# Differential attention normed without 1/sum, its last heads spread over the output projection, and some operands moved by 32 bytes

## The chip, the core and the metric

One NeuronCore of a Trainium2 chip runs the whole program. The metric is device microseconds (us) from start to end of one execution; a kernel's time is the median of several. The engines are named as in the profile: PE is TensorE (PEld its weight loads), DVE is VectorE, ACT is ScalarE, POOL is GpSimd, SP issues the transfers.

## What is computed

A block of three layers over 256 positions of width 1024: a convolution layer, a differential-attention layer (both followed by a cross attention to 256 memory tokens and a SwiGLU of hidden width 2816), then a layer of another kind. The change touches the second layer's attentions and two of the SwiGLUs. Cut to what matters:

```python
# diff_attention: 8 heads, two softmaxes of 64 wide halves, value width 128
p = softmax(where(mask, s, -inf))                 # s = q k / 8, c = 0, 1
a = p[:, :, 0] - lam * p[:, :, 1]
o = einsum('bhqk,bkhe->bqhe', a, v)
o = rms_norm(o, subln_g, 1e-5) * (1.0 - lambda_init)   # per head, over its 128 values
x = x + o.reshape(B, S, 1024) @ w_o

# memory_cross_attention: 4 heads of 256
p = softmax(q k / 16);  o = p @ v;  x = x + o @ w_o

# swiglu
x = x + (silu(h @ w_gate) * (h @ w_up)) @ w_down
```

The norm of a head does not change when the head is multiplied by a positive factor, except through the 1e-5: with unnormed exponentials `e` and their sum `s0` for c = 0, `o = u / s0`, and `o * rsqrt(mean(o^2) + 1e-5)` is `u * rsqrt(mean(u^2) + 1e-5 * s0^2)`.

## The kernel before

**Weights.** Every weight matrix passes as panels of 128 rows by up to 1024 columns. SP loads a panel into `wf` (6 buffers); ACT copies it to `whi` (line 276, the high part in fp32r) and DVE or POOL subtracts, `wlo = wf - whi` (line 278). `whi` and `wlo` have 5 buffers each. Which engine makes `wlo` is told for each matrix by the table `LO`, one letter for each panel in turn (`g` is POOL, `v` is DVE). `consume()` prepares panels up to 5 ahead of the one in use, so a panel's `whi` waits until PE is done with the panel 5 before it.

**Products.** `gemm` (line 409 holds its matmul) multiplies activations, also split into a high and a low part (`S0`, `S1` or `hh`), by the panels: three matmuls for each product, high by high, low by high, high by low. In the form "F" the panel is the stationary operand and 256 positions of the activations stream; in the form "T" the activations are stationary and 512 columns of the panel stream. A panel serves 4 banks of 6 matmuls each. The last `tail` panels are held back and done bank by bank, so that each bank's result can be drained (`evac`) while the next is computed. `hooks` run other work after a given panel.

**Differential attention** is written out in an order by hand. `q` is the projection of two heads, `V` that of the values, `a` the scores and exponentials of a head, `b` the combination of its two halves and its transposes (PE lines 897), `c` the product with the values (lines 906 to 908), and `f` the norm of a pair of heads and its transposes into `S0` (`fin`, lines 913 to 930). `DIFF_SEQ` stands ahead of the output projection; `DIFF_END` hangs the rest on it as hooks: `a6 c4` after panel 0, `a7 c5 b6` after panel 1, `b7 f2 c6 c7 f3` after panel 3. Panels 4 to 7 (`TAIL = 4`) are the held ones. Panel `k` of `w_o` needs head `k`, so panels 4 and 5 need `f2`, panels 6 and 7 `f3`.

In `fin`, four steps on DVE around a power on POOL (line 920) make the factor, DVE multiplies the heads by it (line 925, two instructions of 128x256), and PE transposes (line 928). In the memory attention `b_` DVE scales the exponentials by 1/sum (line 708, two instructions) before PE's transposes (line 712).

**The norm of the layer's input** is applied late: `Stats` adds squares on POOL (line 338), folds them (line 355) and PE sums them over the partitions (line 361). In the projection to `k` (`w_ks`) that sum is asked for after panel 4.

**Where operands lie.** Start addresses in a partition, in bytes, as the built program has them:

| tile | role | start before | modulo 64 |
|---|---|---|---|
| s0h, s0l, s1h, s1l | streaming in form F, stationary in T | 32128, 40320, 48512, 56704 | 0 |
| whi, wlo (10 buffers) | stationary in F, streaming in T | 92256 to 129120 | 32 |
| hh, hl of the first two SwiGLUs | streaming against whi, wlo | 148064, 170592 | 32 |
| hh, hl of the third SwiGLU | stationary, whi and wlo stream | 161408, 183936 | 0 |
| q against memory K; pT against memory V | q stationary, K streams; V stationary, pT streams | all | 32 |

## Time and profile before

| | |
|---|---|
| median of 3 runs | 1169.73 us (1169.61 to 1170.72) |
| the profiled execution's own time | 1166.55 us |
| its span in the profile | 1164.8 us |
| mean granted clock of PE | 0.983 |
| PE busy | 1114.5 us of the span (96%) |
| DVE, ACT, POOL busy | 788.7, 650.2, 426.2 us |

The stages in the order of the span: convolution and memory projections to 182 us, first memory attention to 245, first SwiGLU to 433 (its down projection from 370), differential attention to 559, second memory attention to 623, second SwiGLU to 811 (down projection from 747), then the other layer, whose SwiGLU runs from 973 to the end. Busy shares of the whole span are averages over these; what a part of the change is worth is read in its own stage.

### The profile page before, as it was taken

Reading aid. Unit: us, or ns where it says so; the run is one execution under the profiler, and the core shown is the slowest. Engines: PE = TensorE matmul, PEld = TensorE weight load, DVE = VectorE, ACT = ScalarE, POOL = GpSimd, SP = SyncE. Lnnn points to the kernel's source line nnn. Section 1 sums busy time; section 2 is a strip of 40 time slices with the busy share of each in tenths; the row PEclk is TensorE's granted clock in tenths of the full one; section 3 lists DMA queues with packets and bytes.
Section 4 is the critical chain, followed back from the end, with each engine's and each line's share of the span. In section 5 each row is a group of like instructions: output and inputs, shape, how many; then the busy total and the mean of one; then the engine's idle time right before and its main releaser. Section 6 shows DMA issues by size and latency. Waiting matters only on the chain.

```text
span 1164.8 us, 21545 instructions
## 1 busy us (share of the span) xinstructions
PE 1114.5 (96%) x8418; PEld 1055.0 (91%) x8418; DVE 788.7 (68%) x1445; ACT 650.2 (56%) x1141; POOL 426.2 (37%) x278
## 2 busy tenths in 40 slices
PE   7999989999999999988999999999988998999997
PEld 7998878999999998978899999999887678999986
DVE  6899866596767456675855565745868746887843
ACT  6555476565545355654755554535675745765642
POOL 5999846220000016763726444001663310111300
PEclk9999989999999999998999999999998998999999
DMA  7676535356546544542434654753654015455661
GB/s 265 193 246 206 196 112 179 109 160 207 182 145 235 183 147 165 177 145 73 145 109 134 229 182 149 234 188 102 208 184 160 19 55 176 150 200 155 226 198 37
DMA packets 59799, 191.13 MB, mean 164 GB/s; under 512 B 6752, under 2 KB 10080, under 8 KB 59696
## 3 DMA queue, kind: packets, MB, share of 16 engines
q1 hardware_dynamic: 58288, 187.31, 49.3%
q0 software_dynamic: 688, 1.90, 0.6%
q8 instruction: 66, 1.08, 0.4%
q10 hardware_dynamic: 720, 0.53, 0.1%
q14 instruction: 37, 0.30, 0.1%
HBM read 188.15 MB, written 1.05 MB: 162 GB/s over the span
## 4 chain that ended last, share of the span: by engine, by line
PE 45%; DVE 2%; issue 2%; POOL 1%; ACT 0%; POOLq 0%; DVEq 0%; ACTq 0%
PE acc L409 38%; PE acc L1120 1%; PE acc L1218 1%; PE acc L723 0%; POOL sacc L338 0%; DVE wlo L278 0%; PE acc L1279 0%; PE acc L1283 0%; PE aux L1260 0%; PE acc L1372 0%; PE acc L1280 0%; PE acc L1215 0%; PE acc L1170 0%; POOL sfold L355 0%; PE acc L692 0%
## 5 line engine op out<-in xcount | busy, mean ns | idle before, releaser
L276 ACT ACTIVATE whi<-wf 128x1024 fp32r<-128x1024 f32 (+3 forms) x382 | 371.2, 986 | 310.8 <-PE acc L409 270.2
L278 DVE TENSOR_TENSOR wlo<-wf,whi 128x1024 fp32r<-128x1024 f32 (+3 forms) x251 | 317.5, 1274 | 177.2 <-ACT whi L276 176.3
L278 POOL TENSOR_TENSOR wlo<-wf,whi 128x1024 fp32r<-128x1024 f32 (+1 forms) x131 | 286.9, 2209 | 167.9 <-ACT whi L276 167.6
L409 PE MATMUL acc<-s0h,whi 128*128 128x256 f32 x1192 | 340.0, 286 | 6.0 <-ACT whi L276 5.4
L409 PE MATMUL acc<-s0h,wlo 128*128 128x256 f32 x1192 | 336.9, 283 | 3.4 <-POOL wlo L278 3.4
L409 PE MATMUL acc<-s0l,whi 128*128 128x256 f32 x1192 | 336.6, 283 | 1.7 <-DVE s0l L435 1.7
L409 PEld LDWEIGHTS acc<-s0h,whi 128*128 128x128 f32 x1192 | 228.4, 192 | 7.1 <-ACT whi L276 5.4
L409 PEld LDWEIGHTS acc<-s0h,wlo 128*128 128x128 f32 x1192 | 227.8, 191 | 4.7 <-POOL wlo L278 4.5
L409 PEld LDWEIGHTS acc<-s0l,whi 128*128 128x128 f32 x1192 | 228.3, 192 | 2.7 <-DVE s0l L435 2.1
L409 PE MATMUL acc<-s1h,whi 128*128 128x256 f32 x736 | 205.8, 281 | 0.7 <-ACT s1h L649 0.7
L409 PE MATMUL acc<-s1h,wlo 128*128 128x256 f32 x736 | 205.5, 279 | 0.9 <-POOL wlo L278 0.5
L409 PE MATMUL acc<-s1l,whi 128*128 128x256 f32 x736 | 205.5, 279 | 0.3 <-DVE s1l L435 0.3
L409 PEld LDWEIGHTS acc<-s1h,whi 128*128 128x128 f32 x736 | 138.1, 188 | 1.7 <-ACT s1h L649 1.4
L409 PEld LDWEIGHTS acc<-s1h,wlo 128*128 128x128 f32 x736 | 138.3, 188 | 1.3 <-POOL wlo L278 0.7
L409 PEld LDWEIGHTS acc<-s1l,whi 128*128 128x128 f32 x736 | 138.4, 188 | 0.8 <-DVE s1l L435 0.5
L409 PE MATMUL acc<-hh,whi 128*128 128x256 f32 x352 | 99.6, 283 | 0.0
L409 PE MATMUL acc<-hl,whi 128*128 128x256 f32 x352 | 99.6, 283 | 0.0
L409 PE MATMUL acc<-hh,wlo 128*128 128x256 f32 x352 | 99.6, 283 | 0.0
L338 POOL TENSOR_TENSOR sacc<-sq,sacc 128x512 f32<-128x512 f32 x21 | 33.5, 1596 | 122.4 <-ACT sq L337 122.0
L543 DVE SCALAR_TENSOR_TENSOR aux<-u,vecs,aux 128x256 f32<-128x256 f32 x174 | 68.6, 476 | 1.1 <-ACT aux L541 1.1
L409 PEld LDWEIGHTS acc<-hh,wlo 128*128 128x128 f32 x352 | 67.6, 192 | 0.0
L409 PEld LDWEIGHTS acc<-hl,whi 128*128 128x128 f32 x352 | 67.6, 192 | 0.0
(371 smaller groups left out, 1720.2 us busy)
## 6 DMA issues: line engine op xcount, KB each, us to landing
wf<-in_gu SPq DMA_DIRECT2D x120, 512.0 KB, 3.9
wf<-in_w_down SPq DMA_DIRECT2D x66, 512.0 KB, 4.3
wf<-in_mem_w_k SPq DMA_DIRECT2D x16, 512.0 KB, 4.2
wf<-in_mem_w_v SPq DMA_DIRECT2D x16, 512.0 KB, 3.4
wf<-in_mem_w_q SPq DMA_DIRECT2D x16, 512.0 KB, 3.5
wf<-in_mem_w_o SPq DMA_DIRECT2D x16, 512.0 KB, 4.2
wf<-in_w_pw SPq DMA_DIRECT2D x24, 256.0 KB, 3.1
wf<-in_gv SPq DMA_DIRECT2D x24, 256.0 KB, 2.7
```

What stands on the lines that cost most here:

```text
L276: p["ih"] = SC.activation(p["hi"][:, :W], p["f"][:, :W], AF.Copy)
L278: p["il"] = eng.tensor_tensor(p["lo"][:, :W], p["f"][:, :W], p["hi"][:, :W].bitcast(F32), op=OP.subtract)
L338: self.ins = self.eng.tensor_tensor(self.acc, sq, self.acc, op=OP.add)
L409: PE.matmul(o, l, r, start=(ki == 0 and n == 0 and q == 0), stop=(ki == K - 1 and q == 2), skip_group_check=True)
L543: V.scalar_tensor_tensor(cv[:, c] if k == TAPS - 1 else ai, src, w, ai, op0=OP.mult, op1=OP.add)
L1120: PE.matmul(ph[0:60, 0:256], win[:, a, 4 * g + j], w[:, j * 256:(j + 1) * 256], start=(g == 0 and j == 0 and w is p["hi"]), stop=(g == 3 a ...
L1218: PE.matmul(f, q1, kk[:, kv], start=True, stop=True, skip_group_check=True)
```

## The change

Five things are edited. (1) `b_` of the differential attention keeps `e0 = 1e-5 * s0^2` in the place of `r0 = 1/s0`; `fin` takes one DVE step ahead of the power in the place of three, none behind it, and ACT scales the heads (four instructions of 128x128) in the place of DVE. (2) `DIFF_END` spreads the last heads: `c6` after panel 2, `f2 b7` after bank 1 of panel 3, `c7` after bank 0 of panel 4, `f3` after bank 1 of panel 5; two panels are held in the place of four. (3) The low parts of `w_o` and of the first `q` go from POOL to DVE. (4) In the second memory attention ACT scales the exponentials by 1/sum, in the place of DVE. (5) A tile `pad` of 32 bytes heads the pools of both memory attentions and of the first two SwiGLUs: hh and hl then start at 148096 and 170624 (0 modulo 64), q and pT at 0 modulo 64, while the memory K and V, whi and wlo stay at 32 modulo 64. The first memory attention keeps its scaling on DVE.

```diff
-DIFF_END = {0: "a6 c4", 1: "a7 c5 b6", 3: "b7 f2 c6 c7 f3"}
+DIFF_END = {0: "a6 c4", 1: "a7 c5 b6", 2: "c6", (3, 1): "f2 b7", (4, 0): "c7", (5, 1): "f3"}
...
-          dn0="v", K="v", q="g", V="g", o="g", mq1="gvv", mo1="vgv", gu1="gv", gv1="v",
+          dn0="v", K="v", q="g", V="g", o="v", mq1="gvv", mo1="vgv", gu1="gv", gv1="v",
...
-            declare("w_q", 2 * int(w[1]), 2, nk=4, lo=LO["q"])
+            declare("w_q", 2 * int(w[1]), 2, nk=4, lo="v" if w == "q0" else LO["q"])
...
                 for b in range(len(banks)):
                     mm(ki, cur, b)
+                    for f in hooks.get((ki, b), []):
+                        f()
...
             P = es.enter_context(tc_pool(name=f"ma{i}", bufs=3))
+            V.memset(P.tile([128, 8], F32, name="pad", bufs=1), 0.0)
             P1 = es.enter_context(tc_pool(name=f"mq{i}", bufs=1))
             if i:
+                V.memset(P1.tile([128, 8], F32, name="pad"), 0.0)
...
                 for t in range(2):
-                    V.tensor_scalar(p[:, t], p[:, t], sm[:, 2 + t:3 + t], None, op0=OP.mult)
+                    if i:
+                        SC.activation(p[:, t], p[:, t], AF.Copy, scale=sm[:, 2 + t:3 + t])
+                    else:
+                        V.tensor_scalar(p[:, t], p[:, t], sm[:, 2 + t:3 + t], None, op0=OP.mult)
...
             P = es.enter_context(tc_pool(name=f"ff{i}", bufs=1))
+            V.memset(P.tile([128, 8], F32, name="pad"), 0.0)
...
-            V.reciprocal(r0[:, :, h], sm[:, 0, 0:2])
+            V.scalar_tensor_tensor(e0[:, :, h], sm[:, 0, 0:2], 1e-5, sm[:, 0, 0:2], op0=OP.mult, op1=OP.mult)
...
-            V.tensor_tensor(ms, ss[:, :, hs], r0[:, :, hs], op=OP.mult)
-            V.tensor_tensor(ms, ms, r0[:, :, hs], op=OP.mult)
-            V.tensor_scalar(ms, ms, 1.0 / 128, 1e-5, op0=OP.mult, op1=OP.add)
+            V.scalar_tensor_tensor(ms, ss[:, :, hs], 1.0 / 128, e0[:, :, hs], op0=OP.mult, op1=OP.add)
             rr = small.tile([128, 2, 2], F32, name="orr", tag="orr")
             G.tensor_tensor(rr, ms, mhalf[:, 0:4].rearrange("p (a b) -> p a b", a=2), op=OP.pow)
-            V.tensor_tensor(rr, rr, r0[:, :, hs], op=OP.mult)
             pt = acc()
             for t in range(2):
-                ov = o[:, t, 256 * g:256 * g + 256].rearrange("p (h e) -> p h e", h=2)
-                V.tensor_tensor(ov, ov, rr[:, t, :, None].to_broadcast([128, 2, 128]), op=OP.mult)
                 for i in range(2):
                     h = 2 * g + i
+                    ov = o[:, t, h * 128:(h + 1) * 128]
+                    SC.activation(ov, ov, AF.Copy, scale=rr[:, t, i:i + 1])
                     PE.transpose(pt[:, i * S + t * 128:i * S + (t + 1) * 128], o[:, t, h * 128:(h + 1) * 128], ident)
...
-             hooks={k: [lambda w=w: run(w.split())] for k, w in DIFF_END.items()}, tail=TAIL)
+             hooks={k: [lambda w=w: run(w.split())] for k, w in DIFF_END.items()}, tail=2)
```

A scheduler lays the instructions of each engine in a row; line numbers below 660 grow by 2, those of `fin` by about 5. On POOL, from the last adds of squares of the first SwiGLU through the differential attention (`sacc`, `sfold` and `rr` are the norm of the input, `orr` the power in `fin`), the row before is:

```order
L338 TENSOR_TENSOR sacc<-sq,sacc 128x512 x2
L278 TENSOR_TENSOR wlo<-wf,whi 128x1024
L338 TENSOR_TENSOR sacc<-sq,sacc 128x512
L355 TENSOR_TENSOR sfold<-sacc 128x256
L372 TENSOR_TENSOR rr<-ms,mhalf 128x2
L278 TENSOR_TENSOR wlo<-wf,whi 128x1024 x14
L920 TENSOR_TENSOR orr<-oms,mhalf 128x4
L278 TENSOR_TENSOR wlo<-wf,whi 128x1024 x4
L920 TENSOR_TENSOR orr<-oms,mhalf 128x4
```

and now, to the last `orr`:

```order
L338 TENSOR_TENSOR sacc<-sq,sacc 128x512 x3
L355 TENSOR_TENSOR sfold<-sacc 128x256
L372 TENSOR_TENSOR rr<-ms,mhalf 128x2
L278 TENSOR_TENSOR wlo<-wf,whi 128x1024 x13
L926 TENSOR_TENSOR orr<-oms,mhalf 128x4
L278 TENSOR_TENSOR wlo<-wf,whi 128x1024
L926 TENSOR_TENSOR orr<-oms,mhalf 128x4 x2
L278 TENSOR_TENSOR wlo<-wf,whi 128x1024
L926 TENSOR_TENSOR orr<-oms,mhalf 128x4
```

The low part between the adds is gone, and so are the eight of `w_o` around the powers; one, of the next matrix, stands ahead of the last power.

On ACT, from a square of `c5` (`sqs`) to the start of the drain of `w_o` (`s1h`), with `pT` the copy of `b7` and `s0h` the high part that `f2` and `f3` write, the row before is:

```order
L910 ACTIVATE sqs,ss<-aux 128x128
L276 ACTIVATE whi<-wf 128x1024 x2
L899 ACTIVATE pT<-aux 128x384
L929 ACTIVATE s0h<-acc,subg 128x512
L910 ACTIVATE sqs,ss<-aux 128x128 x4
L929 ACTIVATE s0h<-acc,subg 128x512
L434 ACTIVATE s1h<-acc,vecs 128x256 x3
```

and now, behind the first two scalings of `f2` (`o`), to the last one of `f3`:

```order
L276 ACTIVATE whi<-wf 128x1024
L918 ACTIVATE sqs,ss<-aux 128x128
L932 ACTIVATE o<-o,orr 128x128
L918 ACTIVATE sqs,ss<-aux 128x128
L932 ACTIVATE o<-o,orr 128x128
L934 ACTIVATE s0h<-acc,subg 128x512
L907 ACTIVATE pT<-aux 128x384
L276 ACTIVATE whi<-wf 128x1024
L918 ACTIVATE sqs,ss<-aux 128x128 x2
L932 ACTIVATE o<-o,orr 128x128 x3
L276 ACTIVATE whi<-wf 128x1024
L932 ACTIVATE o<-o,orr 128x128
```

The scalings have come in, and weight copies and the squares of `c6` stand among them.

## Rows read from the trace of the kernel before

**Rows 1.** The page, part 1: busy time, share and instructions of each engine.
```profile
PE 1114.5 (96%) x8418; PEld 1055.0 (91%) x8418; DVE 788.7 (68%) x1445; ACT 650.2 (56%) x1141; POOL 426.2 (37%) x278
```
**Rows 2.** Stretches: length, busy us (count) PE, PEld, DVE, ACT, POOL; PE clock; DMA, GB/s.
```profile
269.00:369.00 100.00, 100.00 (x860) 100.00 (x859) 66.55 (x88) 51.31 (x70) 0.00 (x0) 1.00 0.54 175
370.00:433.00 63.00, 63.00 (x527) 63.00 (x526) 32.32 (x35) 27.17 (x34) 0.00 (x0) 1.00 0.57 185
83.00:105.00 22.00, 22.00 (x96) 17.74 (x95) 21.87 (x51) 11.85 (x16) 21.92 (x11) 1.00 0.62 202
516.60:558.80 42.20, 35.89 (x260) 34.34 (x260) 27.41 (x63) 19.02 (x51) 15.24 (x8) 0.88 0.22 76
```
**Rows 3.** The chain that ended last, second memory attention: start, us, what.
```profile
584.85 5.61 PE acc L409 x48
...
590.46 1.43 PE acc L692 x12
...
603.37 1.43 PE acc L723 x12
```
**Rows 4.** Instructions in order of time, POOL, then PE, `w_ks`: start, us, idle before.
```profile
445.82 2.38 POOL L278 TENSOR_TENSOR wlo<-wf,whi 128x1024 fp32r<-128x1024 f32 x1 [0.36 <-ACT whi L276]
448.17 1.25 POOL L338 TENSOR_TENSOR sacc<-sq,sacc 128x512 f32<-128x512 f32 x1
449.50 0.72 POOL L355 TENSOR_TENSOR sfold<-sacc 128x256 f32<-128x256 f32 x1
...
450.28 0.60 PE L361 MATMUL aux<-ones,sfold 128*128 128x1 f32 x4 [2.76 <-POOL sfold L355]
```
**Rows 5.** Instructions in order of time around `w_o`: POOL, DVE, PE, then ACT.
```profile
515.26 2.49 POOL L278 TENSOR_TENSOR wlo<-wf,whi 128x1024 fp32r<-128x1024 f32 x1 [0.34 <-ACT whi L276]
...
515.42 2.94 DVE L925 TENSOR_TENSOR o<-o,orr 128x256 f32<-128x256 f32 x2
...
539.61 2.91 DVE L925 TENSOR_TENSOR o<-o,orr 128x256 f32<-128x256 f32 x2
...
548.94 0.76 DVE L925 TENSOR_TENSOR o<-o,orr 128x256 f32<-128x256 f32 x2
...
518.17 0.68 PE L928 MATMUL acc<-cst,o 128*128 128x128 f32 x4 [1.23 <-DVE o L925]
...
521.12 0.99 PE L897 MATMUL aux<-cst,p 128*128 128x128 f32 x3 [1.94 <-DVE p L892]
...
542.58 0.69 PE L928 MATMUL acc<-cst,o 128*128 128x128 f32 x2 [2.04 <-DVE o L925]
...
545.92 0.28 ACT L910 ACTIVATE sqs<-aux 128x128 f32<-128x128 f32 x1 [0.51 <-PE aux L908]
...
546.50 0.19 ACT L910 ACTIVATION_READ_ACCUMULATOR sqs<-aux 128x1 f32 x1
```
**Rows 6.** Single microseconds of PE: length, busy (count), granted clock, DMA, GB/s.
```profile
522.00:523.00 1.00, 1.00 (x7) 0.50 0.95 381
...
545.00:546.00 1.00, 1.00 (x6) 0.50 0.05 21
```
**Rows 7.** Instructions in order of time, first softmax of the second memory attention: DVE, PE.
```profile
581.84 2.41 DVE L708 TENSOR_SCALAR p<-p,sm 128x256 f32<-128x256 f32 x2
...
584.04 0.81 PE L712 MATMUL aux<-cst,p 128*128 128x128 f32 x4 [3.57 <-DVE p L708]
```
**Rows 8.** Groups by line and shape: busy us, mean ns of one, idle before.
```profile
L276 ACT ACTIVATE whi<-wf 128x1024 fp32r<-128x1024 f32 x314 | 327.6, 1058 | 266.7 <-PE acc L409 233.3 <-issue 22.4 <-POOL wlo L278 4.3
L278 DVE TENSOR_TENSOR wlo<-wf,whi 128x1024 fp32r<-128x1024 f32 x215 | 286.7, 1342 | 160.9 <-ACT whi L276 159.9
...
L788 ACT ACTIVATE t<-t 128x256 f32<-128x256 f32 x44 | 18.2, 414 | 12.3 <-DVE t L787 11.8
...
L452 ACT ACTIVATE x<-acc 128x512 f32<-128x512 f32 x20 | 11.9, 597 | 0.0
...
L920 POOL TENSOR_TENSOR orr<-oms,mhalf 128x4 f32<-128x4 f32 x4 | 4.1, 1028 | 10.7 <-DVE oms L918 10.7
```

More of the change, by code (lines that the diff above doesn't have):

```diff
@@ L861, in program @@
         B = {}
-        r0 = P1.tile([128, 2, 8], F32, name="r0")
+        e0 = P1.tile([128, 2, 8], F32, name="e0")
         ss = P1.tile([128, 2, 8], F32, name="ss")
```

## The prediction

> **What bounds the kernel now.** I read the page's busy times first: PE works in 96% of the span, no other engine in more than 68% [rows 1]. Only two things can then move the end: the time PE takes for a matmul, and the few stretches in which PE stands idle or slow. For the first I read stretches of pure matmul [rows 2]. In the gate and up part of the first SwiGLU 860 matmuls of 256 columns take 100 us, 116.3 ns each; in its down projection 527 of the same shape take 63 us, 119.5 ns each. In both, PE is busy throughout at a granted clock of 1.00, so the 3.3 ns are no wait. The operands lie differently: `hh` streams at 32 modulo 64 against `whi` at 32, while the faster stretch streams tiles at 0 against the same `whi`. The chain of waits has the same pair once more [rows 3]: 48 matmuls of the projection take 5.61 us (116.9 ns each), while the two memory-attention products, both operands at 32, take 1.43 us for 12 (119.2 ns each). For the second I read the output projection of the differential attention as one stretch: PE is busy for 35.89 of 42.20 us at a mean clock of 0.88 [rows 2]. Then the instructions in order of time give each idle time its releaser [rows 4, 5, 7].
>
> **Operands moved by 32 bytes.** Each pair that has both operands at 32 now has one at 0 and one at 32. With the tile at 0 streaming that is the faster stretch; with the tile at 0 stationary and the panel at 32 streaming (the new way round for the memory V or K against q and pT included), 96 matmuls of 512 columns take 22 us, 229 ns each, under two of the fast 256-column ones [rows 2]. So I take the full difference: two down projections of 22 panels by 4 banks by 6 are 1056 matmuls by 3.26 ns, 3.4 us; two memory attentions with 4 heads of 24 are 192 by 2.3 ns, 0.4 us. **Gain 3.8 us.** Bounds: 0, if another cause than the address slows these stretches, and 4.1 if the fast stretch's edges are counted in. The `pad` memsets are tiny and stand on DVE, which is idle for a third of the span [rows 1]; they cost nothing while PE has queued matmuls, and some 0.2 us each if not. The Trainium skill speaks against this gain (rivals).
>
> **Low parts moved from POOL: the norm of the layer's input.** PE waits 2.76 us for the fold before it sums over the partitions [rows 4]. On POOL's row a `wlo` of 2.38 us stands between the last two adds and pushes the second, of 1.25, and the fold, of 0.72, behind it. Without it, the add can start when its squares are there instead. POOL had been kept from it for at most the 2.38, and the squares that release it come later than the `wlo`'s start, so I take half: **gain 1.2 us**, bounds 0 and 2.76. What is late next is that add itself, and the `wlo`, now on DVE: 1.34 us of it [rows 8] beside POOL, with DVE free there.
>
> **The output projection.** What is there to win: 42.20 − 35.89 = 6.3 us idle, of which 1.23, 1.94 and 2.04 stand in front of `f1`, `b5` and the second half of `f2` [rows 5]; and the clock, (1 − 0.88) × 42.2 × 0.85 busy = 4.3 us. The microseconds at half clock, 7 and 6 matmuls in each in the place of 8.6, come right after `f1` with `b5` and after `f2` [rows 2, 6], behind those idle times. The pair of DVE scalings takes 2.94 and 2.91 us beside a `wlo` on POOL, 0.76 us at `f3` [rows 5]: so sharing with POOL, not the work, made DVE late, and both causes go (no `wlo` of `w_o` on POOL, no scaling on DVE). What is put in their place I add up by laying the new rows of PE, ACT and POOL against one another:
> - `f1`: the power, 1.03 us [rows 8], then the scalings of 128x128, 0.28 each by the square of that shape [rows 5]. 0.7 us of PE's wait stays; `b5`'s exponentials aren't behind the scaling any more, so 1.94 goes.
> - `f2` on ACT's row: power 1.03, four scalings 1.1, a `whi` of 1.06 [rows 8] and a square pair between, 0.6: 3.8 us. PE has 12 matmuls of panel 3 and the first transposes over it, 1.7. Wait 2.1.
> - `f3`: squares of `c7` 0.77 (545.92 to 546.69) [rows 5], power 1.03, four scalings 1.1, two `whi` 2.1, DVE's step and the handovers some 0.7: 5.7 us, with 30 matmuls (3.5 us) between `c7` and `f3`. Wait 2.2.
> - The drain: with two held panels a bank has 12 matmuls, 1.4 us, in the place of 2.8; ACT needs about 2 × 0.41 + 2 × 0.60 = 2.0 for a bank [rows 8]. PE, which goes on with the next matrix, waits 0.8 at the last ones.
> - Smaller waits that I find in the same comparison: 0.5 at the rotation of `q3`, 0.45 at `b6` and `c6`, 0.5 for the low part that follows `f2` and `f3`. None lasts long enough to slow the clock by what `f1` before shows, where the loss came behind 1.23 and 1.94 in a row.
>
> Together 7.25 us. I take the clock as full. **Gain 6.3 + 4.3 − 7.25 = 3.4 us**, bounds −1 (clock lost again) and 8 (ACT finds cover for both). Eight low parts of `w_o`, 1.34 us each, go on DVE, which is busy for 27.4 of 42.2 us there [rows 2]; they fit, if they don't stand ahead of what PE waits for (third rival). Queued behind ACT's scalings is the `whi` of the next panels, and PE behind that has several panels ready.
>
> **The scaling in the second memory attention.** The pair takes DVE 2.41 us at the first head, and PE waits 3.57 in all for it [rows 7]. ACT does 128x256 in 0.41 [rows 8]. The first transpose waits for the first scaling only; by my rows it can start about **1.0 us** sooner, since the sum and its inverse, ahead of both, stay. Bounds 0 and 2.41. For the later heads PE has matmuls and doesn't wait, so nothing there.
>
> **The sum:** 3.8 + 1.2 + 3.4 + 1.0 = 9.4 us off the profiled execution's 1166.55 us, 1157.15. The median of the runs lies 1169.73 − 1166.55 = 3.2 us above that execution; with that, 1160.3 us.
>
> **Rivals.**
> *The pads do nothing.* The rows show that two stretches differ and that the addresses differ with them, not that one causes the other; the down projection also has 22 panels where the other has 8. Against this rival: the memory products, with other shapes and stages, have the same 2.3 to 3.3 ns [rows 3], and the pairing divides all stretches that I read. Then 9.4 − 3.8 = 5.6: 1164.1 us. Chance 0.12. The Trainium skill, "TensorE: Matmul & The Clock Gate", in "Step-by-step: what each phase is for", says that PE has two independent read ports and that a load of the next weights takes no read bandwidth from the running matmul; by that rule the place of an operand couldn't matter. The trace's 116.3 against 119.5 ns does not settle that.
>
> *The half clock stays.* `f2` and `f3` now each make PE wait for some 2 us, as `f2` did before (2.04), behind which the half-clock microseconds stand [rows 5, 6]. If both bring it back, the 4.3 us are lost again: 9.4 − 4.3 = 5.1, 1164.6 us. For it: the lengths are alike. Against it: at `f1` the half clock came behind two waits within 3 us (518.17 and 521.12 [rows 5]), and the new waits stand alone, with 3.5 us and more of work between them. Chance 0.13.
>
> *DVE becomes late, slower than before.* The eight low parts, 8 × 1.34 = 10.7 us, are laid in DVE's row among the masked scores, combinations and copies. If each stands ahead of a step that PE waits for, and the clock stays half, then 9.4 − 4.3 − 10.7 = −5.6: 1175.3 us. It decides from the fourth panel of the eight (5.1 / 1.34 = 3.8), and measurably from the sixth. Against it: DVE has 14.8 us free there and PE has panels prepared ahead. Chance 0.04.
>
> **How the numbers follow.** The forecast, 1160.3 us, has 0.67; the three rivals 0.12, 0.13, 0.04; a larger gain, below 1155, 0.04. 0.2% (2.3 us) is about what a measurement of this kernel can tell from no change, so the same ends at 1167.4 and 1172.1. The forecast's own terms at their bounds reach from 1165 (the projection at −1) to 1155 (its 8 with half of the others' tops); the first two rivals lie inside that. The range is 1155.0 to 1165.5. Outside 1167.4 are the third rival's 0.04 and a joint failure of two terms of the sum, 0.05: faster 0.91, same 0.05, slower 0.04.
>
> **What would show it.** Right: 116.3 to 116.9 ns in both down projections (528 of them: 63.1 us become 61.4 to 61.7) and in the memory products; a wait for the fold of about 1.6 us in `w_ks`; no 0.50 clock in the output projection, with two waits of about 2 us ahead of `f2`'s and `f3`'s transposes, released by ACT; the first transposes of the second memory attention behind some 2.6 us. Wrong: 119.5 ns as before (the address isn't the cause); 0.50 behind `f2` and `f3`; waits of PE released by DVE's masked scores or copies, behind a `wlo`; a transfer or a weight copy that PE waits for in the output projection, since ACT's row there has grown by the scalings of three `fin` while its copies stand among them.

## The result, and the profile after

The changed kernel takes 1156.21 us (median of 4 runs, 1154.35 to 1157.34), against 1170.07 us of before beside it. The ratio is 0.9865 (95% interval 0.984 to 0.989). Between the medians lie 13.9 us; the ratio makes it 15.8 of the 1169.7 shown before (12.9 to 18.7), and the two profiled executions, 1166.55 and 1154.35 us, differ by 12.2. The forecast was 9.4. The sign was right and all three figures are larger than the forecast, the one between the medians by about a half. The ratio puts the changed kernel at 1153.9 us, below the range's 1155.0; its own median of 1156.21 lies just inside.

The tables of stages in this part are worked out in one way: PE's instructions stand in nearly the same order in all these kernels, so a stage lasts from the start of one matmul to the start of another at the same places of PE's order. The output projection starts with the last matmul ahead of `f1`'s transposes, so the wait ahead of them is in it. Of the two profiled executions (the two rows of the differential attention share one forecast):

| stage | before, us | after, us | difference | forecast |
|---|---|---|---|---|
| to the first memory attention | 176.9 | 178.1 | +1.2 | 0 |
| that attention, first gate and up part | 187.4 | 187.0 | −0.4 | −0.2 |
| first down projection | 63.4 | 61.6 | −1.8 | −1.7 |
| `w_ks` past the fold | 18.2 | 17.0 | −1.2 | −1.2 |
| differential attention up to `f1` | 65.5 | 65.5 | 0.0 | −3.4 with the next |
| `f1` to the end of `w_o` | 42.1 | 33.0 | −9.1 | |
| second memory attention | 64.3 | 63.9 | −0.4 | −1.2 |
| second gate and up part | 124.1 | 124.1 | 0.0 | 0 |
| second down projection | 63.4 | 61.6 | −1.8 | −1.7 |
| the rest, up to the last down projection | 286.4 | 287.4 | +1.0 | 0 |

The last down projection and what follows it take 67.8 us in both.

Part 1 of the page, busy time, share of the span and instructions of each engine, answers [rows 1]:

```profile
PE 1107.7 (96%) x8418; PEld 1048.2 (91%) x8418; DVE 782.6 (68%) x1432; ACT 658.0 (57%) x1165; POOL 403.2 (35%) x268
```

PE still sets the end. Its 8418 matmuls are the same ones, and it is busy 6.8 us less. The stretches, with the columns of [rows 2] (length; busy us and count of PE, PEld, DVE, ACT, POOL; PE's clock; DMA share, GB/s), are the gate and up part, the down projection and the output projection:

```profile
268.00:368.00 100.00, 100.00 (x859) 100.00 (x858) 66.72 (x89) 51.21 (x70) 0.00 (x0) 1.00 0.52 171
371.00:432.00 61.00, 61.00 (x525) 61.00 (x525) 31.95 (x35) 26.83 (x33) 0.00 (x0) 1.00 0.58 197
514.57:547.72 33.15, 31.83 (x261) 30.56 (x259) 23.06 (x55) 21.83 (x61) 4.42 (x3) 1.00 0.40 128
```

The down projection now takes 61/525 = 116.2 ns a matmul, as the stretch above it does. The output projection is the surprise: PE is idle for 1.3 us of it, where it had been for 6.3, and the clock is 1.00 throughout, where its mean had been 0.88. In order of time, with the idle time and its releaser in brackets, PE's waits in the changed stages are:

```profile
448.27 0.61 PE L361 MATMUL aux<-ones,sfold 128*128 128x1 f32 x4 [1.49 <-POOL sfold L355]
...
531.36 0.33 PE L933 MATMUL acc<-cst,o 128*128 128x128 f32 x1 [0.17 <-ACT o L932]
...
538.53 0.91 PE L933 MATMUL acc<-cst,o 128*128 128x128 f32 x3 [0.24 <-ACT o L932]
...
540.35 0.33 PE L933 MATMUL acc<-cst,o 128*128 128x128 f32 x1 [0.91 <-ACT o L932]
...
559.28 0.60 PE L361 MATMUL aux<-ones,sfold 128*128 128x1 f32 x4 [0.43 <-POOL sfold L355]
...
563.22 0.58 PE L696 MATMUL acc<-memK1h,ql 128*128 128x256 f32 x1 [2.28 <-DVE ql L591]
```

Against [rows 4, 5, 7]: the fold's wait is 1.49 in the place of 2.76, as forecast. `f1` and `b5` have no wait left, `f2` (531.36) has 0.17, `f3` (538.53, 540.35) 0.24 and 0.91. The 3.57 us ahead of the second memory attention's transposes are gone, but 2.28 us have come up some 10 us earlier, ahead of the scores of its first head.

### The profile page after: what moved, and what is told of

It reads as the page before. It is cut to its first block, busy times and chain, and to the rows that moved or that the text cites. A ratio compares the mean times of both kernels' runs of the same rounds, so it can differ in the third digit from the quotient of the medians.

```text
span 1152.5 us, 21545 instructions
## 1 busy us (share of the span) xinstructions
PE 1107.7 (96%) x8418; PEld 1048.2 (91%) x8418; DVE 782.6 (68%) x1432; ACT 658.0 (57%) x1165; POOL 403.2 (35%) x268
## 4 chain that ended last, share of the span: by engine, by line
PE 46%; ACT 2%; DVE 2%; issue 2%; POOL 1%; POOLq 0%; DVEq 0%; ACTq 0%
PE acc L409 38%; PE acc L1125 1%; PE acc L1223 1%; ACT whi L276 1%; PE acc L696 1%; PE acc L730 0%; POOL sacc L338 0%; PE acc L1284 0%; PE acc L1288 0%; DVE wlo L278 0%; PE aux L1265 0%; PE acc L1377 0%; DVE memK1l L587 0%; PE acc L1285 0%; PE acc L1220 0%
## 5 line engine op out<-in xcount | busy, mean ns | idle before, releaser
L278 DVE TENSOR_TENSOR wlo<-wf,whi 128x1024 fp32r<-128x1024 f32 (+2 forms) x261 | 327.8, 1264 | 183.7 <-ACT whi L276 178.3
L278 POOL TENSOR_TENSOR wlo<-wf,whi 128x1024 fp32r<-128x1024 f32 (+1 forms) x121 | 261.8, 2186 | 164.7 <-ACT whi L276 162.6
L409 PEld LDWEIGHTS acc<-hh,whi 128*128 128x128 f32 x352 | 66.2, 188 | 0.0
```

The source lines that it names most:

```text
L278: p["il"] = eng.tensor_tensor(p["lo"][:, :W], p["f"][:, :W], p["hi"][:, :W].bitcast(F32), op=OP.subtract)
L409: PE.matmul(o, l, r, start=(ki == 0 and n == 0 and q == 0), stop=(ki == K - 1 and q == 2), skip_group_check=True)
```

## Operands moved by 32 bytes, taken apart

**32 bytes alone.** The edit is the pads of the change, in the kernel before:

```diff
+            V.memset(P.tile([128, 8], F32, name="pad", bufs=1), 0.0)    # mem_attention
+                V.memset(P1.tile([128, 8], F32, name="pad"), 0.0)       # its second one
+            V.memset(P.tile([128, 8], F32, name="pad"), 0.0)            # swiglu
```

> The kernel before with the pads of 32 bytes alone. Theory (two operands that lie at the same remainder of 64 bytes cost a 256-column matmul some 3 ns): both down projections fall from 63.4 to 61.6 us, the memory products from 119.5 to 117 ns, in all 3.8 us off: 1166.3 against 1170.1. Rival (the address is not the cause, the trace of the changed kernel has the shorter stages from something else): 63.4 us stays, 1170.

It gave a ratio of 0.9968 (0.9948 to 0.9988), which is 3.7 us off (1.4 to 6.1), and both down projections at 61.60 us. The first one, in the columns of the stretches above:

```profile
371.00:431.00 60.00, 60.00 (x516) 60.00 (x516) 30.93 (x35) 25.82 (x32) 0.00 (x0) 1.00 0.58 194
```

60/516 is 116.3 ns. The pads make the shorter stages: no other part of the change is in this kernel, and the runs without pads below keep 63.4.

**64 bytes.** The same pads with `[128, 16]`, so that `hh` and the panels are both at 32 modulo 64 again.

> The same pads with 64 bytes in the place of 32: every tile moves, the memsets are there, but hh, hl, q and pT stay at 32 modulo 64, as whi, wlo and the memory K and V. Theory: no gain, 63.4 us in both down projections, 1170. Rival (it is the distance moved or the order of the pools that counts, not the remainder): 61.6 us and 1166.

Neither came. The stage got shorter still, 59.85 us:

```profile
373.00:432.00 59.00, 59.00 (x523) 59.00 (x522) 31.48 (x35) 26.43 (x33) 0.00 (x0) 1.00 0.60 201
```

59/523 is 112.8 ns (113.3 over the whole stage; the count of a stretch takes in the matmuls that straddle its ends, so from here on a stage's own length over its matmuls is given). So the remainder of 64 is the wrong ruler. `hh` lies 0 bytes modulo 512 from `whi` before, 32 in the changed kernel and 64 here, and the matmul takes 120.0, 116.7 and 113.3 ns. The whole kernel gained less than these 7 us: 0.9986 (0.9965 to 1.0007). In its profiled execution PE ran at half clock at four places behind waits from `w_ks` to the second memory attention, where before it had done so at two (the last part comes back to this).

**The panels moved.** 32 bytes ahead of `whi` and `wlo` alone:

```diff
     ring = ctx.enter_context(tc_pool(name="ring", bufs=NB_PANEL))
+    V.memset(ring.tile([128, 8], F32, name="pad", bufs=1), 0.0)
```

> The kernel before with 32 bytes ahead of whi and wlo alone: whi, wlo, hh of the first two SwiGLUs, memory K, V, q and pT all move from 32 to 0 modulo 64, where S0 and S1 lie already, so that nearly every 256-column product has both operands at 0. Theory (the same remainder is slow, whichever): the down projections stay at 63.4 us and the other 256-column products against whi and wlo, 5784 in number, go from 116.7 to 120 ns, up to 19 us slower: 1180 to 1189. Rival (only operands at 32 are slow, those at 0 are fast): all at 116.7, 3.8 us faster, 1166.

1.0119 (1.0087 to 1.0152), 14 us slower. The gate and up part, whose operands now are both at 0, and the down projection, where `hh` moved along with the panels:

```profile
268.00:368.00 100.00, 100.00 (x836) 100.00 (x835) 64.71 (x87) 49.35 (x69) 0.00 (x0) 1.00 0.50 163
375.00:437.00 62.00, 62.00 (x519) 62.00 (x518) 31.23 (x35) 26.22 (x32) 0.00 (x0) 1.00 0.55 185
```

Both at 119.5 to 119.6 ns. It isn't an address that is slow, but the distance between the two operands. The Trainium skill, "TensorE: Matmul & The Clock Gate", "Step-by-step: what each phase is for", has PE read the streaming operand and the next weights through two independent ports, so that the load takes no read bandwidth from the running matmul. These runs speak against the rule as far as time goes: the same matmuls in the same order take 113 to 120 ns, by where one operand lies against the other. Whether it is the load that takes bandwidth from the running matmul, no run shows.

**Two scans**, to see the whole curve: the changed kernel with pads of many sizes.

```diff
+    V.memset(ring.tile([128, 24], F32, name="pad", bufs=1), 0.0)             # second scan: 40
-            V.memset(P.tile([128, 8], F32, name="pad"), 0.0)                 # swiglu
+            V.memset(P.tile([128, (32, 24)[i]], F32, name="pad"), 0.0)       # second scan: (48, 64)
```

> The changed kernel with other pads: 96 bytes ahead of whi and wlo, so that S0 and S1 lie 192 bytes modulo 256 from them (288 before); hh of the first SwiGLU 128 bytes modulo 512 from the panels, hh of the second 96; q and pT 64 bytes from the memory K and V in both memory attentions. Known so far: 120.0 ns at 0, 116.7 at 32, 113.3 at 64. Theory P (the cost repeats every 128 bytes and is least at 64): S0 and S1 products 113.3 ns, first down projection 120 (63.4 us), second 116.7 (61.6 us), memory products 113.3; 5784 products by 3.4 ns less 1.8, about 18 us off the changed kernel's 1156: 1138. Rival G (it goes on falling by 3.3 ns for every 32 bytes): first down projection 106.7 ns (56.3 us), second 110 (58.1), S products 106.7 or less: 1156 - 58 - 9 = 1090. Rival 0 (only the 60 us of one stage were odd): S products stay at 116.7, 1156.

> The same with 160 bytes ahead of whi and wlo (S0 and S1 128 bytes modulo 256 away), hh 192 and 256 bytes modulo 512 away, q and pT 160 bytes away in the first memory attention and 96 (modulo 128) in the second. Theory P (repeats every 128, least at 64): S products 120 ns, both 888-matmul stages 106.6 us in the place of 103.7; first down projection 113.3 ns (59.8 us), second 120 (63.4 us); memory products 116.7. Rival G (goes on falling): 56 us or less in the down projections.

First scan: the convolution's projection, the first gate and up part, and both down projections; second scan: the first gate and up part and both down projections.

```profile
106.00:127.00 21.00, 21.00 (x188) 21.00 (x187) 20.75 (x54) 10.99 (x13) 21.00 (x11) 1.00 0.65 212
266.00:366.00 100.00, 100.00 (x852) 100.00 (x851) 66.03 (x88) 50.65 (x70) 0.00 (x0) 1.00 0.52 170
371.00:433.00 62.00, 62.00 (x519) 62.00 (x518) 31.29 (x35) 26.20 (x32) 0.00 (x0) 1.00 0.55 183
739.00:801.00 62.00, 62.00 (x519) 62.00 (x519) 29.74 (x32) 25.82 (x34) 1.29 (x1) 1.00 0.51 161
```

```profile
270.00:370.00 100.00, 100.00 (x845) 100.00 (x845) 65.28 (x88) 50.00 (x68) 0.00 (x0) 1.00 0.51 168
376.00:434.00 58.00, 58.00 (x515) 58.00 (x514) 30.43 (x34) 25.73 (x31) 0.00 (x0) 1.00 0.59 195
744.00:806.00 62.00, 62.00 (x519) 62.00 (x518) 29.72 (x32) 25.78 (x34) 1.29 (x1) 1.00 0.49 159
```

With the stage's length over its number of matmuls, and the distance as the streaming operand's address less the stationary one's:

| distance of `hh` from the panels, bytes modulo 512 | 0 | 32 | 64 | 96 | 128 | 192 | 256 |
|---|---|---|---|---|---|---|---|
| ns a matmul in the down projection | 120.0 | 116.7 | 113.3 or 117.8 | 120.0 | 120.0 | 113.3 | 120.0 |

So it doesn't go on falling (rival G), and 0, 128 and 256 are alike, as 64 and 192 are: as far as these distances go, it repeats every 128 bytes, with the least at 64. Theory P fails in two places. At 96 I expected the 116.7 of 32. And the gate and up part of the first scan, at 64, takes 117.9 ns over its 888 matmuls where the convolution's projection, at the same distance modulo 128, takes 113.4; the one of the second scan, at 0 modulo 128, takes 118.8. The first scan's whole time, 1149.43 us and 0.9803 (0.978 to 0.9826), against 1138 expected, is this failure for the most part: two gate and up parts 4.1 us and a down projection 1.8 us longer than theory P has them make 10 of the 11. The second scan took 1161.11 in its one timed run.

That 64 bytes give either time is shown best by a later run (the last of "Better versions"), whose two down projections have the same addresses:

```profile
370.00:430.00 60.00, 60.00 (x512) 60.00 (x512) 30.90 (x34) 25.27 (x32) 0.00 (x0) 1.00 0.59 199
740.00:799.00 59.00, 59.00 (x522) 59.00 (x521) 29.75 (x32) 26.90 (x36) 3.17 (x6) 1.00 0.52 162
```

512 in 60 us and 522 in 59: 117.8 and 113.3 ns over the stages. What sets which of the two stays open; the addresses do not. The down projections at the change's 32 bytes took 116.7 in all six profiles that have them there, but that distance has two times as well. In two profiled executions of the changed kernel itself, one of the convolution's projections (its operands are 288 bytes apart, 32 modulo 128) took 117.8 ns in one and 116.7 in the other, over the same 115 matmuls without a wait:

```profile
69.00:82.00 13.00, 13.00 (x112) 13.00 (x112) 13.00 (x35) 5.04 (x5) 13.00 (x7) 1.00 0.66 228
```

```profile
69.00:82.00 13.00, 13.00 (x114) 13.00 (x113) 13.00 (x34) 5.23 (x6) 13.00 (x7) 1.00 0.69 224
```

## The output projection, taken apart

**All three edits without the pads and without ACT's scaling in the second memory attention**: low parts, `fin` on ACT, new order.

> The change without the pads and with the second memory attention's scaling left on DVE: the low parts, the scalings of fin on ACT and the new order alone. By the forecast's terms 1.2 + 3.4 = 4.6 us off: 1165.5. By what the changed kernel's trace shows (waits of only 0.17 and 1.15 us at f2 and f3 in the place of 7.25, clock full): 1.2 + 9.4 = 10.6 off, 1159.5. If part of that came from the pads or the other scaling, between the two.

0.9884 (0.9856 to 0.9912), 13.6 us off; in the profiles, from `w_ks` to the end of `w_o`, 115.4 us against 125.8. Those 10.3 us are the trace's reading (10.6), not the forecast's 4.6. Then each alone, in the kernel before.

**Low parts of `w_o` and the first `q` on DVE:**

```diff
-          dn0="v", K="v", q="g", V="g", o="g", ...
+          dn0="v", K="v", q="g", V="g", o="v", ...
-            declare("w_q", 2 * int(w[1]), 2, nk=4, lo=LO["q"])
+            declare("w_q", 2 * int(w[1]), 2, nk=4, lo="v" if w == "q0" else LO["q"])
```

> The kernel before with the low parts of w_o and of the first q on DVE alone. Theory W (DVE's scalings take 2.9 us only because a wlo runs beside them on POOL, 0.76 without): the fold's wait in w_ks falls from 2.76 to 1.5 us, the scalings at f1 and f2 to about 0.8 us, the four idle times around w_o from 6.3 to about 3 us, with less half clock: 5 to 7 us off. Rival (third rival of the forecast, DVE becomes late by eight low parts of 1.34 us): no gain beyond the 1.2 of w_ks, or slower.

**`e0` and the scalings of `fin` on ACT** (the hunks of `b_` and `fin` of the change):

```diff
-                V.tensor_tensor(ov, ov, rr[:, t, :, None].to_broadcast([128, 2, 128]), op=OP.mult)
+                    SC.activation(ov, ov, AF.Copy, scale=rr[:, t, i:i + 1])
```

> The kernel before with e0 and the scalings of fin on ACT alone (low parts stay on POOL, old order). Theory W: the first transposes of f1 and f2 follow the power by some 0.6 us, b5's exponentials have DVE for themselves: idle times around w_o from 6.3 to about 2 us and the clock full behind f1, 6 to 8 us off. Forecast's count of waits: f1 0.7, f2 2.1, f3 2.2 stay, so idle 5 us and 1 to 2 us off.

**The new order and two held panels:**

```diff
-DIFF_END = {0: "a6 c4", 1: "a7 c5 b6", 3: "b7 f2 c6 c7 f3"}
+DIFF_END = {0: "a6 c4", 1: "a7 c5 b6", 2: "c6", (3, 1): "f2 b7", (4, 0): "c7", (5, 1): "f3"}
```

> The kernel before with the new order of the last heads and two held panels alone. Theory W (the waits come from slow steps on DVE and POOL, not from the order): f1 and b5 keep 1.23 and 1.94 us, f2 and f3 wait about 2 us each for DVE's scalings: within 2 us of before. Rival (the order is what hides the waits): f2 and f3 without waits, 5 us off.

**The changed kernel with the old order** (that hunk taken back, four held panels):

> The changed kernel with the old order of the last heads and four held panels. The low parts alone and the scalings alone each took the output projection from 41.8 to 34 us, the order alone only to 40.1, and it brought the 2.29 us wait ahead of the second memory attention's scores. Theory N (once either of the other two is there, the order is worth nothing or less): stage 34 to 34.5 us, the 2.28 us wait is gone and the one ahead of the transposes is back at about 2.6 us (3.5 less the 0.9 of ACT's scaling): within 1 us of the changed kernel's 1156. Rival (the order hides what is left): f2 and f3 wait 2 us each, 3 to 4 us slower, 1160.

| kernel | ratio (interval) | `w_ks` past the fold, us | to `f1` | `f1` to the end of `w_o` | second memory attention |
|---|---|---|---|---|---|
| before | | 18.2 | 65.5 | 42.1 | 64.3 |
| low parts alone | 0.9887 (0.986 to 0.9914) | 16.9 | 67.2 | 33.5 | 65.9 |
| `fin` on ACT alone | 0.9914 (0.9888 to 0.994) | 18.2 | 65.5 | 32.9 | 65.8 |
| order alone | 0.9959 (0.9935 to 0.9982) | 18.2 | 65.5 | 40.3 | 64.8 |
| all three | 0.9884 (0.9856 to 0.9912) | 16.9 | 65.5 | 33.0 | 64.8 |
| changed kernel | 0.9847 (0.9823 to 0.9871) | 17.0 | 65.5 | 33.0 | 64.0 |
| changed, old order | 0.9843 (0.982 to 0.9867) | 17.0 | 65.5 | 32.4 | 64.3 |

(The row of the changed kernel is a second profile and timing of it, beside the old order on one chip. The 67.2 us have a stretch at half clock behind the fold's wait. The 41.8, 34 and 40.1 us that the expectation of the old order names were counted to places that differ by some matmuls between the kernels; those of the table are the same in all.)

> The changed kernel once more, beside the three others on one chip: 1154 to 1157.

The low parts and the scalings are worth nearly the same alone, 8.7 and 9.2 us in the stage, and both in the old order 9.8: each ends the same collision, an instruction of DVE beside a `wlo` on POOL. In their ratios they are worth more than was expected, 13.2 us for 5 to 7 and 10.1 for 6 to 8; what the profiled stages do not show of that stays open. The scaling of `f1` on DVE with the low parts moved, and the only two waits left in `w_o` there, on PE:

```profile
517.59 0.75 DVE L925 TENSOR_TENSOR o<-o,orr 128x256 f32<-128x256 f32 x2
...
523.42 0.46 PE L874 MATMUL acc<-k,q 128*128 128x128 f32 x2 [0.78 <-DVE q L843]
...
542.77 0.44 PE L928 MATMUL acc<-cst,o 128*128 128x128 f32 x2 [0.96 <-DVE o L925]
```

0.75 us in the place of 2.94 [rows 5], with five `wlo` on DVE between the first line and the last. PE waits for none of them itself, but the first (518.98, 1.22 us) stands in DVE's row ahead of the `q` that PE waits 0.78 us for. The Trainium skill, "Perfetto Trace Analysis", "Optimizing Scalar/DVE Operations", says that GpSimd and DVE share a read port; by that the two instructions of 128x256 would have to wait for POOL's `wlo`, and here the trace agrees: 2.94 us beside it, 0.75 without. With the scalings on ACT and the low parts still on POOL, PE's one wait of that kind is at `f3`:

```profile
539.71 0.33 PE L925 MATMUL acc<-cst,o 128*128 128x128 f32 x1 [1.04 <-ACT o L924]
```

With the order alone the old waits stand where they were, that of `f2` at 2.13, only `f3` has none, and the one ahead of the second memory attention's scores has come:

```profile
519.14 0.68 PE L930 MATMUL acc<-cst,o 128*128 128x128 f32 x4 [1.23 <-DVE o L927]
...
522.08 0.99 PE L899 MATMUL aux<-cst,p 128*128 128x128 f32 x3 [1.94 <-DVE p L894]
...
541.11 0.77 PE L930 MATMUL acc<-cst,o 128*128 128x128 f32 x4 [2.13 <-DVE o L927]
...
573.45 0.58 PE L694 MATMUL acc<-memK1h,ql 128*128 128x256 f32 x1 [2.29 <-DVE ql L591]
```

The stage gains 1.8 us, but the ratio 4.8 (2.1 to 7.6), more than the 2 that theory W allowed; the rest of that is in no stage of its profile. Without the order the changed kernel waits 0.93 us at `f3` and nothing at `f2`, and then ahead of the memory attention's transposes again:

```profile
537.82 0.33 PE L933 MATMUL acc<-cst,o 128*128 128x128 f32 x1 [0.93 <-ACT o L932]
...
571.33 0.43 PE L719 MATMUL aux<-cst,p 128*128 128x128 f32 x1 [1.93 <-ACT p L713]
...
572.21 0.90 PE L719 MATMUL aux<-cst,p 128*128 128x128 f32 x3 [0.45 <-ACT p L713]
```

1155.28 against 1155.53 us beside it: the spreading of the last heads is worth nothing that can be measured once the collision is gone.

## The second memory attention

**ACT's scaling taken back** in the changed kernel, to `V.tensor_scalar`.

> The changed kernel with the scaling of the second memory attention back on DVE. By the forecast the first transposes come 1.0 us later. By the changed kernel's trace (there the transposes follow without a wait, and PE waits 2.28 us ahead of the scores instead, for the low part of q, which no scaling precedes): no difference over 0.5 us from the output projection to the end of that attention.

The kernel took 1158.25 us in its one run, and the stage 64.8 us, against 63.9 and 64.0 in the two profiles of the changed kernel: 0.8 us, by two profiles of one and one of the other. That is nearer to the forecast's 1.0 than to my reading of no difference. In the old order the gain stands at the wait itself: 3.47 us ahead of the first transposes with `fin` alone, 1.93 and 0.45 above.

Why DVE was slow there shows in the kernel before. The first pair of scalings, 2.41 us at 581.84 [rows 7], runs beside a `wlo` on POOL; the second head's has no POOL instruction beside it:

```profile
581.49 2.34 POOL L278 TENSOR_TENSOR wlo<-wf,whi 128x1024 fp32r<-128x1024 f32 x1
...
588.72 0.62 DVE L708 TENSOR_SCALAR p<-p,sm 128x256 f32<-128x256 f32 x2
```

So this too looks like the collision of the output projection; whether moving this one `wlo` would have done as well as moving the scalings, no run shows.

Against the kernel before the stage gains only 0.4 us, because it begins with a new wait, with half clock behind it, and because the profile of before has full clock behind its 3.57 us (last section). The new wait is the 2.28 us above, and 2.27 in the run with all three edits and no scaling on ACT: so not this edit made it but the new order. DVE and POOL ahead of it, in the changed kernel:

```profile
556.23 6.33 DVE L587 TENSOR_TENSOR memK1l<-memK,memK1h 128x512 fp32r<-128x512 f32 x4 [1.13 <-ACT memK1h L585]
559.70 2.86 DVE L587 TENSOR_TENSOR memK1l<-memK,memK1h 128x512 fp32r<-128x512 f32 x1
562.48 0.68 DVE L591 TENSOR_TENSOR ql<-acc,qh 128x512 fp32r<-128x512 f32 x1
...
559.27 2.74 POOL L278 TENSOR_TENSOR wlo<-wf,whi 128x1024 fp32r<-128x1024 f32 x1
```

It is the same collision once more. The last of the four steps on the memory K (128x512), the second line, takes 2.86 us beside a `wlo` on POOL, where `ql` of the same size takes 0.68 behind it, and `ql` is what PE waits for.

**`w_q`'s low parts off POOL**, all but the first:

```diff
-          ... mq1="gvv", ...
+          ... mq1="gvvvvvvv", ...
```

> The changed kernel with the low parts of the second memory attention's w_q on DVE, all but the first. Theory W (the 2.28 us wait of PE for the low part of q, and the half clock behind it, come from DVE's memory-K steps that run beside POOL's wlo and fold): without POOL's wlo the last memory-K step falls from 2.86 to about 0.7 us, the wait goes, full clock: 2 to 3.5 us off, 1153 against 1156. Rival (the wlo takes the same place on DVE, 1.3 us each, ahead of the low part of q): wait stays at 2 us or grows, 1156 to 1157.

0.9831 (0.9808 to 0.9853), 1152.42 us. The stage takes 62.3 us. DVE gets to `ql` at 560.87, before PE, and the next wait is 1.51 us at the transposes:

```profile
559.14 1.81 DVE L587 TENSOR_TENSOR memK1l<-memK,memK1h 128x512 fp32r<-128x512 f32 x2
560.87 0.68 DVE L591 TENSOR_TENSOR ql<-acc,qh 128x512 fp32r<-128x512 f32 x1
...
571.57 0.94 PE L719 MATMUL aux<-cst,p 128*128 128x128 f32 x4 [1.51 <-ACT p L713]
```

So theory W holds: the stage is 1.6 us shorter than in the changed kernel. PE's idle time in it falls from 2.7 to 2.1 us, and the stretch at half clock behind the old wait, to which I put the other 1.0, is not in this profile.

## Better versions

Three more runs put the findings together: distances of 64 bytes and `w_q`'s low parts on DVE, with the panels moved by 96 bytes (first), where they were (second), and the second with the old order (third).

> The changed kernel with the low parts of the second memory attention's w_q on DVE but for the first, 96 bytes ahead of whi and wlo, and 64 bytes in the place of 32 in the pads of both first SwiGLUs, the first memory attention and the second one's K: every pair of operands 64 bytes apart modulo 128. By the runs so far: 3.8 us off the changed kernel for the low parts, 3.5 for the down projections (59.8 us each), 4 for the third SwiGLU and 2 for the convolution's projections, some 2 us lost in the gate and up parts (117.8 ns with this ring, 116.7 without): 1145 to 1147. If the gate and up parts come to 113.4 with hh at 64: 1139.

> The changed kernel with w_q's low parts on DVE and pads of 64 bytes in the place of 32 (but for the 32 ahead of the second memory attention's q), whi and wlo where they were. Theory (operands 64 bytes apart modulo 128 take 113.3 ns, where whi and wlo are at 96 modulo 128 as in the run with 64-byte pads): both down projections 59.8 us, gate and up parts 103.7 each: 3.8 + 3.5 + 0.3 off 1156, 1148.5. Rival (the 62.2 us of the last run belong to 64 bytes beside the other edits): 62.2 us each, 1153.

> The last one with the old order of the last heads and four held panels. Theory N: no difference to it from w_ks to the second SwiGLU over 1 us. Rival: 3 us slower in the output projection.

The first gave 1145.33 us, 0.9763 (0.9738 to 0.9787), and is the fastest of all, some 11 us under the changed kernel's median on another chip and 27 under the kernel before that ran beside it. Its first gate and up part took 113.4 ns a matmul (884 in 100 us), its second, at the same distance, 117.9 (852 in 100), and both down projections 117.8 ns. So the total came as expected by luck: the down projections lost 4.8 us against the 59.8 expected of each, and the first gate and up part gained 3.9.

```profile
264.00:364.00 100.00, 100.00 (x884) 100.00 (x884) 69.08 (x91) 53.76 (x73) 0.00 (x0) 1.00 0.57 181
...
623.00:723.00 100.00, 100.00 (x852) 100.00 (x851) 61.62 (x73) 50.07 (x70) 35.95 (x15) 1.00 0.56 178
```

The second gave 0.9819 (0.9795 to 0.9842), 1152.08, with both down projections at 59.84 us as its theory has it; the total is 3.6 us above the 1148.5 expected, and why is not shown. The third gave 0.9819 (0.9793 to 0.9844), 1152.81. They are within their intervals of each other, so the old order is again no slower. In the third's profile the output projection took 32.3 us (33.0 in the second), and the memory attention 64.7 (62.0), behind waits of 2.32 and 1.44 us ahead of its transposes: what the order costs at one place it gives back at the other, and in these two profiles more.

## Why the prediction was right or wrong

**What bounds the kernel** was read rightly: PE, with its time a matmul, its waits and the clock behind them. What the runs could assign lies in these.

**The pads** were right in size, 3.5 us in the two down projections for 3.4, and the 32-byte run shows them as the cause; the first rival falls. The memory products gained a little less than their 0.4: but for the first that stream `pT`, 12 in a row came 119.1 to 120.0 ns apart before and, where PE has no wait in them, 116.4 to 119.1 in the changed kernel, some 0.3 us over the 192 of them. The rule behind the pads, one operand at 0 and one at 32 modulo 64, was only argued from three stages, and it is wrong: 64 bytes leave both at the same remainder, and the down projections were faster still. It picked the right answer by luck, because all pairs of before that I had read lay at two distances only.

**The fold** in `w_ks`: 1.49 us for a forecast 1.56, right, and 1.48 in the run with the low parts alone. That half of the 2.38 us would be won was a guess, and its size is luck. POOL's last add starts 0.14 us after its squares (445.64 and 445.50) in the place of 1.94 (448.17 and 446.23), but it takes 1.77 us in the place of 1.25, beside the `wlo` that now stands on DVE (445.05 to 446.28).

**The output projection** is the step that failed: 3.4 us forecast, 9.1 measured. The part to be won (6.3 idle, 4.3 of clock) was right, and it came. The term that was mis-sized is the 7.25 us of waits put in its place; 1.3 are there. At `f2` I counted 3.8 us of power, scalings and weight copy from the moment at which PE enters panel 3. In the trace the power of `f2` begins before that:

```profile
527.53 1.01 POOL L926 TENSOR_TENSOR orr<-oms,mhalf 128x4 f32<-128x4 f32 x1 [14.88 <-DVE oms L924]
...
528.58 0.69 ACT L932 ACTIVATE o<-o,orr 128x128 f32<-128x128 f32 x2
529.17 1.05 ACT L276 ACTIVATE whi<-wf 128x1024 fp32r<-128x1024 f32 x1
...
530.92 0.39 ACT L932 ACTIVATE o<-o,orr 128x128 f32<-128x128 f32 x1
...
530.70 0.49 PE L933 MATMUL acc<-cst,o 128*128 128x128 f32 x3
```

Its release is `c5`'s squares, a panel and a half earlier, and PE reaches the transposes at 530.70, when two of the four scalings are done and the third is about to end. The chain's length was right (527.53 to 531.31 is 3.8 us) and its start was not. At `f3` the chain that I gave 5.7 us is there too, behind `c7`, and costs 1.15 of the 2.2, since three transposes no longer wait for the fourth scaling. The waits of 0.4 to 0.8 at `f1`, `q3`, `b6` and the drain came to nothing: each was the sum of durations of one engine without asking whether the row had begun earlier. The second rival (half clock behind `f2` and `f3`) falls: the waits are 0.17 and 1.15 us, and the clock is full behind them. Of the third, the eight low parts on DVE, the run with the low parts alone shows one that stands ahead of a step of PE, for a wait of 0.78 us; in the changed kernel that wait is not there.

The forecast priced the three parts of that edit as one and held both the low parts and the scalings to be needed. The runs show that either alone ends the collision, and that the order is worth nothing beside the two.

**The second memory attention**: the gain of 1.0 at the transposes is 0.8, but the stage is only 0.4 shorter. I looked for what is late next at the transposes, and not at what comes ahead of them when PE arrives with the chain of DVE and POOL behind it: DVE and POOL set the waits at the start of the stage, and a PE that reaches it in another order waits elsewhere. The "rest" of +1.0 us and the start of +1.2 belong to no edit that I can name; no run settles them. The same 904 matmuls behind the second down projection took from 159.5 to 164.2 us in the profiles of kernels that differ only ahead of them.

## What to carry to other kernels

An instruction of DVE that takes three times as long as its twin elsewhere was here, in all three places, one with a `wlo` of POOL beside it; ask for that before moving work to a third engine, since either move cures it and the second cure adds little. When a new chain is laid against an engine that waits for it, count from the release of its first step, not from the place where the waiting engine stands in the code. And where matmuls run back to back, compare their spacing between stages: a few nanoseconds times thousands are microseconds, and a pad of some bytes tries for them. Look at more than one execution, since the same addresses gave two spacings.

## What was not expected of the hardware

The time of a 256-column matmul depends on the distance between its operands' addresses: 120.0 or 118.8 ns at 0 modulo 128 bytes, 116.7 or 117.8 at 32, 113.3 or 117.8 at 64, 120.0 at 96.

The clock behind a wait differs from run to run, at the same wait. Ahead of the transposes of the second memory attention PE is idle for 3.57 us before [rows 7], 3.71 in the run with 32 bytes alone and 3.58 in that with the low parts alone; this is what follows in the three:

```profile
585.00:587.00 2.00, 2.00 (x19) 2.00 (x19) 2.00 (x4) 0.49 (x1) 0.00 (x0) 1.00 0.90 274
```

```profile
585.00:587.00 2.00, 2.00 (x11) 2.00 (x11) 0.73 (x3) 1.20 (x4) 0.00 (x0) 0.50 0.80 229
```

```profile
578.00:580.00 2.00, 2.00 (x12) 2.00 (x11) 2.00 (x4) 0.60 (x1) 0.00 (x0) 0.55 0.80 252
```

19 matmuls in two microseconds at 1.00, 11 and 12 at half. So a wait of that length costs its own time and, in some executions, some 1.5 us more (the stage takes 64.3, 65.8 and 65.9 us in the three), which may be why a kernel that loses its waits gains more in its median than its waits were long. In the 64-byte run half clock follows the fold's 2.99 us as well, where the 2.76 of before was followed by full clock. The length of the wait alone does not decide it: behind the fold's 1.48 us in the run with the low parts alone the clock is half (0.50 from 452 to 454), behind the 1.49 of the changed kernel it is full. What decides it, I have not found.
